# A two-layer decoder trunk on one core: transfers issued by SyncE in the order of the source

## The chip, the cores and the metric

The kernel runs on one core of one Trainium2 chip. The metric is device time in microseconds (us) of one execution. The engines named below: TensorE (PE, its weight loads PEld), VectorE (DVE), ScalarE (ACT), GpSimd (POOL) and SyncE (SP), whose only work here is to issue transfers (DMAs) and to read page numbers into its registers. All 976 transfers of this kernel are issued by SP, which the profile lists as SPq.

## The reference, cut to what matters

A prompt of 1024 rows and 8 sample rows (one new token each, 4096 earlier tokens in a paged cache) go through two layers:

```
layer 0: p = x @ w_in_ab                       # 1024 -> 3072: q, k, v, g_a, u_b, g_b
         o_a = stick_breaking(q, k, v)         # z = q k^T / 8 + bias, weights sigmoid(z) * prod(1 - sigmoid)
                                               # sample rows: k, v also from cache_k[page_table], cache_v[page_table]
         o_b = multiscale_pool(u_b) @ w_pool * pool_scale
         x = layer_norm(ALPHA * x + [o_a * silu(g_a), o_b * silu(g_b)] @ w_out_ab)
layer 1: a, a_gate, gate = split(x @ w_in_c)   # 1024 -> 3072
         h = a * sigmoid(a_gate)
         c = silu(layer_norm(depthwise_conv31(h) + b_dw))
         x = layer_norm(ALPHA * x + (c * silu(gate)) @ w_out_c)
```

Besides the rows it returns the new k and v, the last 15 rows of u_b, and the last 30 rows of h (`conv_prompt`, for the prompt). The cache of K and that of V are read as 256 pages each, one page (128 tokens x 512, 256 KB) per transfer, at addresses taken from `page_table`.

## The kernel before, in words

**Arithmetic.** A float32 product is made of three matmuls on a high and a low part: hi*hi, lo*hi, hi*lo (`project`, lines 225 to 227; `out_group`, lines 1034 to 1036). Weights come as float32 (`dma_w`, L200, tile `wraw`, 3 buffers), ACT copies the high part (L205, `whi`), POOL or DVE subtracts for the low part (L210, `wlo`). A half block of weights is 512 rows by 128 columns, 256 KB.

**Stages.** (1) Start: rows are loaded and transposed, first weights are split, small vectors are turned (`setup_small`, L479 on). (2) Input projection of layer 0 with attention, pooling and, beside it, the K pages of the cache (`decode_k`, L405 load, L417 POOL product, L409 DVE sum). (3) Output projection of layer 0 (`out_layer`). (4) From about 600 to 930 us the "V stage": the input projection of layer 1 on PE (`c_gen`, a generator over column blocks), the depthwise convolution on DVE (L1385) and, in part, on ACT and POOL (`head`, L1372 and L1375, tile `tap`), and on PE beside these the V pages (`decode_v`, L1161 load, L1163 matmuls, 9 buffers `vt`). (5) A middle piece, about 930 to 985 us: statistics, norm and gate of layer 1, with the sample rows (`sample_path`). (6) Output projection of layer 1.

**What sets the order.** One Python program calls small steps of several generators in turn: `fill.part()` is one piece of the projection (six matmuls in the V stage), `tick()` one step of `decode_k`, `decode_v` or `sample_path`, and `point()` counts down functions put off by `defer(n, fn)`, which run n points later. `manual_schedule` (L170) names the engines whose instructions keep the order in which this program calls them: PE, ACT, DVE and POOL. SP is not among them: a scheduler of the framework sets the order in which SP issues. SP issues one transfer after another; where one has to wait (for the data that it stores, or for a buffer to come free), all behind it wait too.

**Steps that the change touches.** `blocks_gen` (L229) and `c_gen` (L267) fetch half blocks of weights ahead. `tail_rows` (in `conv`, L1392 on), once for each of the 8 column blocks of layer 1, transposes the last 30 rows of h on PE (L1394), lets ACT copy them into the tile `hst` (L1396) and stores `hst` to `conv_prompt` (L1397); `hst` shares its two buffers (tag "sq") with `tap`. In `decode_v` SP reads two page numbers of each of four sequences (`page_ids`, L352, listed as TENSOR_LOAD of `pt`) and then issues 8 page loads, enough for two ticks; a tick is 4 page matmuls. `store_queries` (L382) writes the sample queries to memory (`q_dram`), from which `query_rows` (L386) reads them back. `sample_path` loads the sample rows (tile `sA`, L1249), norm vectors (L1214) and the first weight rows (`issue`, L1191, tile `vt`).

Of the kernel before, what the change touches and what calls it, by code (L numbers as in the profile page):

```python
# [24 lines left out]
P = 128  # L25
D = 1024
S = 1024
NB = 8
# [72 lines left out]
def kernel(  # L101
# [67 lines left out]

    ctx.enter_context(tc.manual_schedule(engines={ENG.PE, ENG.Activation, ENG.DVE, ENG.Pool}))  # L170
    bdw, cng, cnb = pvec[:, 0, :], pvec[:, 1, :], pvec[:, 2, :]
# [5 lines left out]
    def defer(n, fn):  # L177
        deferred.append([n, fn])
# [50 lines left out]
    def blocks_gen(blocks, chunks, tiles, when, lead):  # L229
        def src(bi, i):  # L230
            w, f0 = blocks[bi][0], blocks[bi][1]
            return w[i * 512:(i + 1) * 512, f0:f0 + P]

        stream = [(bi, i) for bi in range(1, len(blocks)) for i in range(2)]
        raws = []

        def ahead():
            if stream:
                raws.append(dma_w(src(*stream.pop(0)), 4, P))

        for _ in range(lead):
            ahead()

        def advance():
            if raws:
                nxt.append(conv_w(raws.pop(0), 4, P))
                ahead()

        for bi, b in enumerate(blocks):
            nxt = []  # L250
            for c, (c0, n) in enumerate(b[4] if len(b) > 4 else chunks):
                o = acc()[:, 0:n]
# [12 lines left out]
            tiles = nxt  # L265

    def c_gen(blocks, tiles):  # L267
# [5 lines left out]

        def fetch(bi):
            if bi < len(blocks):
                w, f0 = blocks[bi][0], blocks[bi][1]
                raws[bi] = [dma_w(w[i * 512:(i + 1) * 512, f0:f0 + P], 4, P) for i in range(2)]

        def ready(bi, i):
            if bi in raws:  # L280
                tiles.setdefault(bi, []).append(conv_w(raws[bi][i], 4, P))

        for s, (bi, c) in enumerate(items):
# [4 lines left out]
            if s == 1:  # L288
                fetch(2)
            elif s > 3 and c == 0 and bi < end:  # L290
                fetch(bi + 1)
            o = acc()[:, 0:n]
            for k in range(NK):
                project(o, tiles[bi], k, c0, n)
                if k in (1, 3, 5):
                    if s == 3 and k < 5:
                        ready(2, k // 2)
                    elif 3 < s and bi < end and (c, k) in ((0, 5), (1, 1)):
                        ready(bi + 1, c)
                    elif (bi, c, k) == (end - 1, 1, 3):  # L300
                        fetch(end + 1)
                    elif (bi, c) == (end, 0) and k < 5:
                        ready(end + 1, k // 2)
                    point()
                    yield None
# [294 lines left out]
    def evac_k(pair):  # L600
        fs = slice(pair * P, (pair + 1) * P)

        def f(c, c0, n, o):
# [7 lines left out]
            dve.tensor_tensor(out=kl, in0=o, in1=km[:, 0].bitcast(F32), op=ALU.subtract)  # L611
            sp.dma_start(km[DH:P, 1].bitcast(F32), km[DH:P, 0].bitcast(F32))
            sp.dma_start(km[0:DH, 1].bitcast(F32), kl[DH:P].bitcast(F32))

            def dup():
                sp.dma_start(km[DH:P, 0].bitcast(F32), kl[0:DH].bitcast(F32))
            defer(2, dup)

            def g():
# [8 lines left out]
                sp.dma_start(kp_out[c0:c0 + m * P, fs].rearrange("(t p) f -> p t f", p=P),  # L628
                             kst[:, 0:m * P].rearrange("p (t f) -> p t f", f=P))
                if c == 2:  # L630
                    krow = ab.tile([P, P], F32, tag="row", name="krow", bufs=3)
                    act.activation(out=krow[0:NB], in_=t[0:NB, 256:384], func=AF.Copy)
                    sp.dma_start(ks_out[:, fs], krow[0:NB])
            defer(2, g)
        return f

    def evac_v(pair):
        fs = slice(pair * P, (pair + 1) * P)

        def f(c, c0, n, o):  # L640
# [6 lines left out]
            def g():  # L647
# [8 lines left out]
                if c == 2:  # L656
                    vrow = ab.tile([P, P], F32, tag="row", name="vrow", bufs=3)
                    act.activation(out=vrow[0:NB], in_=t[0:NB, 256:384], func=AF.Copy)
                    sp.dma_start(vs_out[:, fs], vrow[0:NB])
                    sp.dma_start(vp_out[:, fs].rearrange("(t p) f -> p t f", p=P), vn)  # L660
            defer(2, g)
# [14 lines left out]
    def evac_u(g):  # L676
# [3 lines left out]
        def f(c, c0, n, o):  # L680
# [30 lines left out]
            def g2():  # L711
# [3 lines left out]
                gp.tensor_tensor(out=hb[:, 0:n], in0=hb[:, 0:n], in1=SGB[g][:, c0:c0 + n], op=ALU.mult)  # L715
                sp.dma_start(hb_dram[g * P:(g + 1) * P, c0:c0 + m], hb[:, 0:m])
                if c == 2:
                    gp.tensor_copy(shs[:, 4 + g, :], hb[:, m:n])
                if c == 2:
# [3 lines left out]
                    act.activation(out=ust[0:23], in_=t[0:23, 0:P], func=AF.Copy)  # L723
                    sp.dma_start(pool_prompt[0, 0, :, g * P:(g + 1) * P], ust[0:PS_, :])
                    sp.dma_start(pool_sample[0, :, PS_ - 1, g * P:(g + 1) * P], ust[PS_:23, :])
            defer(G2LAG, g2)
# [62 lines left out]
    def prep(pair, i):  # L789
# [4 lines left out]
        dve.tensor_tensor(out=ql, in0=q, in1=sq[:, 0].bitcast(F32), op=ALU.subtract)  # L794
        for r in (slice(0, DH), slice(DH, P)):
            sp.dma_start(sq[r, 1].bitcast(F32), sq[DH:P, 0].bitcast(F32))
        defer(2, lambda: sp.dma_start(sq[DH:P, 0].bitcast(F32), sq[0:DH, 0].bitcast(F32)))
        SQ[pair, i] = sq, ql
# [239 lines left out]
    def out_layer(w, first, ahead, X, gb, pool, finish, between, before=None, half=None, tail=None, lag=OLAG, fast0=FAST, wide=0, gps=()):  # L1038
        order = [(n4, tb) for t0 in (0, 4) for n4 in range(2) for tb in range(t0, t0 + 4)]
        for i in range(NTB + lag):  # L1040
            if i < NTB:
                order.append((2, i))
            if i >= lag:
                order.append((3, i - lag))
        dmas = {0: (1, 3)} | {9 + i: (2, i) for i in range(4)} | {13 + i: (3, i) for i in range(4)}
        convs = {i: (1, i) for i in range(4)} | {12 + i: (2, i) for i in range(4)} | {16 + i: (3, i) for i in range(4)}
# [59 lines left out]
    def before0(n4, tb):  # L1106
        if n4 == 0:
            load_res(tb + 2)
        if n4 == 0 and tb == 4:
            sp.dma_start(pool_sample[0, :, 0:PS_ - 1, :], state_pool[0, :, 1:PS_, :])  # L1110
            sp.dma_start(conv_sample[0, :, 0:KS - 1, :], state_conv[0, :, 1:KS, :])
# [18 lines left out]
    def fin0(tb, y, h):  # L1130
        sp.dma_start(x1_dram[tb * P:(tb + 1) * P, h], y[:, h])

        def f():
            for hf in range(h.start // 512, h.stop // 512):
                t = trp()
# [216 lines left out]
    def conv(cb):  # L1352
# [39 lines left out]
        def tail_rows():  # L1392
# [3 lines left out]
            act.activation(out=hst, in_=t[0:KS, 0:P], func=AF.Copy)  # L1396
            sp.dma_start(conv_prompt[0, 0, :, cb * P:(cb + 1) * P], hst)  # L1397

# [304 lines left out]
```

## Time and profile before

| | |
|---|---|
| median of 3 runs | 1111.97 us (1108.72 to 1115.1) |
| profiled execution: its time | 1110.31 us |
| its span, mean granted TensorE clock | 1108.5 us, 0.972 |
| PE busy | 1042.0 us, 94% of the span |
| DVE, POOL, ACT busy | 833.3 us (75%), 632.2 us (57%), 493.4 us (45%) |
| matmuls L225, L226, L227 | 360.3, 338.8, 339.3 us, modelled ends that overlap |
| V page matmuls L1163 | 74.5 us |
| transfers | 235.20 MB, mean 212 GB/s |

The span is the time from the first to the last instruction that the profile shows; the execution's own time is 1.8 us longer. Busy time is an average over stages: in the V stage PE has no idle time worth the name, in the start, at the layer change and in the middle piece it has. SP waits often (for POOL before weight loads, for DVE before K pages, for PE before V pages). Such a wait shows as time of another engine only where that engine wants something that stands behind the waiting transfer.

### The profile page before, as it was taken

To read this page: it belongs to the slowest core of one execution; us is meant where nothing else is said; L and a number is where in the kernel's file an instruction comes from. 1 tells how busy PE (TensorE), PEld (TensorE's weight loads), DVE (VectorE), ACT (ScalarE), POOL (GpSimd) and SP (SyncE) were. 2 spreads that over 40 slices of the span, in tenths; PEclk is the share of its full clock that TensorE was granted. 3 is DMA by queue.
4 is the path that set the end of the run, shared out by engine and by line. 5 is a ranking of instruction groups with operands and counts; after the bars stand their busy time and mean duration, and the time that the engine had idled before them with its cause. 6 is when DMAs were issued, how large, how long until landed. Compare 5 with 4: busy or idle time off the path is not lost.

```text
span 1108.5 us, 19858 instructions
## 1 busy us (share of the span) xinstructions
PE 1042.0 (94%) x6804; PEld 840.1 (76%) x6804; DVE 833.3 (75%) x982; ACT 493.4 (45%) x933; POOL 632.2 (57%) x488
## 2 busy tenths in 40 slices
PE   8899998999999989979988999999999899799996
PEld 7897887888888878979986666566666466678786
DVE  3368899899689988698874699999999960584246
ACT  5245665665766647601143244534543412462111
POOL 3266858567276878568765266757764612342135
PEclk9999999999999989989988999999999999889998
DMA  8577857865457776478425786877687678386933
GB/s 268 171 205 228 253 181 214 257 207 176 131 158 230 243 217 217 151 263 267 155 100 177 218 262 214 267 241 232 208 263 235 205 244 266 111 271 217 321 108 135
DMA packets 179350, 235.20 MB, mean 212 GB/s; under 512 B 15434, under 2 KB 95955, under 8 KB 179225
## 3 DMA queue, kind: packets, MB, share of 16 engines
q1 hardware_dynamic: 179249, 233.94, 67.0%
q8 instruction: 53, 0.87, 0.3%
q14 instruction: 48, 0.39, 0.1%
HBM read 212.60 MB, written 16.14 MB: 206 GB/s over the span
## 4 chain that ended last, share of the span: by engine, by line
PE 51%; POOL 7%; DVE 6%; DMA 5%; issue 2%; ACT 2%; SPq 2%; POOLq 0%; DVEq 0%; ACTq 0%
PE acc L225 10%; PE acc L227 9%; PE acc L226 9%; PE qv L1163 6%; DMA kt<-in_cache_k_dram 3%; POOL kt L417 2%; PE acc L1034 2%; PE acc L1036 2%; PE acc L1035 2%; DVE conv L1581 2%; PE zt L1034 1%; POOL wlo L210 1%; DVE xl L196 1%; PE qv L1199 1%; PE zt L1035 1%
## 5 line engine op out<-in xcount | busy, mean ns | idle before, releaser
L225 PE MATMUL acc<-xh,whi 128*128 128x384 f32 (+2 forms) x960 | 360.3, 375 | 1.9 <-DVE hbt L705 1.4
L227 PE MATMUL acc<-xl,whi 128*128 128x384 f32 (+2 forms) x960 | 339.3, 353 | 0.5 <-DVE xl L196 0.5
L226 PE MATMUL acc<-xh,wlo 128*128 128x384 f32 (+2 forms) x960 | 338.8, 353 | 0.0
L417 POOL TENSOR_TENSOR kt<-kt,qbs 128x1024 f32<-128x1024 f32 x96 | 237.8, 2487 | 79.0 <-DMA kt<-in_cache_k_dram 58.8
L210 POOL TENSOR_TENSOR wlo<-wraw,whi 128x512 fp32r<-128x512 f32 x122 | 163.6, 1345 | 176.6 <-ACT whi L205 154.0
L1385 DVE SCALAR_TENSOR_TENSOR conv_acc<-hbuf,wdwT,conv_acc 128x1024 f32<-128x1024 f32 x196 | 252.8, 1290 | 6.8
L225 PEld LDWEIGHTS acc<-xh,whi 128*128 128x128 f32 x960 | 183.0, 191 | 68.5 <-issue 27.2
L227 PEld LDWEIGHTS acc<-xl,whi 128*128 128x128 f32 x960 | 182.8, 190 | 18.4 <-DVE xl L196 0.9
L226 PEld LDWEIGHTS acc<-xh,wlo 128*128 128x128 f32 x960 | 183.4, 191 | 15.8
L409 DVE TENSOR_REDUCE zw<-kt 128x16 f32<-128x1024 f32 x128 | 152.9, 1211 | 28.0 <-POOL kt L417 23.0
L1375 POOL TENSOR_TENSOR conv<-conv,tap 128x512 f32<-128x512 f32 x84 | 105.9, 1293 | 15.5 <-ACT tap L1372 15.5
L205 ACT ACTIVATE whi<-wraw 128x512 fp32r<-128x512 f32 x126 | 77.6, 625 | 71.9 <-DMA wraw<-in_w_out_ab_dram 55.8
L1034 PE MATMUL acc<-whi,xh 128*128 128x256 f32 x352 | 103.9, 295 | 0.0
L1036 PE MATMUL acc<-whi,xl 128*128 128x256 f32 x352 | 101.0, 287 | 2.2 <-DVE xl L196 2.2
L1035 PE MATMUL acc<-wlo,xh 128*128 128x256 f32 x352 | 100.9, 287 | 0.6 <-POOL wlo L210 0.6
L365 DVE TENSOR_TENSOR_SCAN kp<-kp,zt 128x512 f32<-128x512 f32 (+3 forms) x96 | 92.5, 964 | 6.1 <-ACT zt L361 6.1
L1372 ACT ACTIVATE tap<-hbuf,wdwT 128x512 f32<-128x512 f32 x84 | 59.8, 721 | 46.1 <-POOL conv L1375 37.7
L1163 PE MATMUL qv<-vt,zw 128*32 128x512 f32 x512 | 74.5, 603 | 3.1 <-DMA vt<-in_cache_v_dram 3.1
L360 ACT ACTIVATE kp<-zt,nbiash 128x512 f32<-128x512 f32 (+3 forms) x96 | 55.8, 581 | 46.0 <-PE zt L823 24.5
L1034 PEld LDWEIGHTS acc<-whi,xh 128*128 128x128 f32 x352 | 68.5, 194 | 8.3 <-issue 7.8
L1036 PEld LDWEIGHTS acc<-whi,xl 128*128 128x128 f32 x352 | 68.5, 195 | 2.4 <-DVE xl L196 2.4
L1035 PEld LDWEIGHTS acc<-wlo,xh 128*128 128x128 f32 x352 | 68.5, 195 | 1.1 <-POOL wlo L210 1.0
(286 smaller groups left out, 1501.7 us busy)
## 6 DMA issues: line engine op xcount, KB each, us to landing
kt<-in_cache_k_dram SPq DMA_DIRECT2D x256, 256.0 KB
vt<-in_cache_v_dram SPq DMA_DIRECT2D x256, 256.0 KB
wraw<-in_w_in_c_dram SPq DMA_DIRECT2D x48, 256.0 KB
vt<-in_w_in_c_dram SPq DMA_DIRECT2D x48, 256.0 KB
wraw<-in_w_in_ab_dram SPq DMA_DIRECT2D x46, 256.0 KB
xt<-in_x_prompt_dram SPq DMA_DIRECT2D x8, 512.0 KB
wraw<-in_w_out_ab_dram SPq DMA_DIRECT2D x16, 256.0 KB
xres<-in_x_prompt_dram SPq DMA_DIRECT2D x8, 512.0 KB
```

Source lines behind the costliest of these rows:

```text
L210: (eng or gp).tensor_tensor(out=lo, in0=raw, in1=hi.bitcast(F32), op=ALU.subtract)
L225: pe.matmul(o, hi[:, k % 4, :], xh, start=(k == 0), stop=False)
L226: pe.matmul(o, lo[:, k % 4, :], xh, start=False, stop=False)
L227: pe.matmul(o, hi[:, k % 4, :], xl, start=False, stop=(k == NK - 1))
L409: dve.tensor_reduce(out=seg[:, j // 8, j % 8:j % 8 + 2, bi * 8:bi * 8 + 8], in_=kts.pop(s - KLAG - 1).rearrange("p a (h d) -> p a h d", d=DH),
L417: eng.tensor_tensor(out=kt, in0=kt, in1=qrow[b], op=ALU.mult)
L1034: pe.matmul(o, XH[:, k, cs], hi[:, k % 2, :], start=(k == 0), stop=False)
L1035: pe.matmul(o, XH[:, k, cs], lo[:, k % 2, :], start=False, stop=False)
L1036: pe.matmul(o, XL[:, k, cs], hi[:, k % 2, :], start=False, stop=(k == NK - 1))
L1163: pe.matmul(pv[32 * bi:32 * bi + 32, :], Z[:, j % 8 * 4 + j // 8, :], vts[bi], start=(j == 0), stop=(j == NPG - 1), tile_position=(0, 32 * ...
L1375: gp.tensor_tensor(out=ch, in0=ch, in1=tcs(t), op=ALU.add)
L1385: dve.scalar_tensor_tensor(out=part[1], in0=hb[:, j:j + S], scalar=w, in1=part[1], op0=ALU.mult, op1=ALU.add)
```

## The change

SP is added to the engines with manual order, so that it issues in the order in which the program calls `dma_start`. Many calls are put off by `defer` or moved: the K copies and stores, the pooling stores, the pair copies of the queries, the `hst` stores and the loads of the layer-1 residual; weight half blocks are asked for one at a time rather than two (`fetch(bi, i)`), and a step later. `defer(2, ...)` before the `hst` store means two points after the PE transpose. On PE, ACT, DVE and POOL the order of instructions is unchanged, and the number of transfers is the same (976).

```diff
-    ctx.enter_context(tc.manual_schedule(engines={ENG.PE, ENG.Activation, ENG.DVE, ENG.Pool}))
+    ctx.enter_context(tc.manual_schedule(engines={ENG.PE, ENG.Activation, ENG.DVE, ENG.Pool, ENG.SP}))
...
         def advance():
+            if not raws:
+                ahead()
             if raws:
                 nxt.append(conv_w(raws.pop(0), 4, P))
-                ahead()
+                defer(3, ahead)
...
-        def fetch(bi):
-            if bi < len(blocks):
-                w, f0 = blocks[bi][0], blocks[bi][1]
-                raws[bi] = [dma_w(w[i * 512:(i + 1) * 512, f0:f0 + P], 4, P) for i in range(2)]
+        def fetch(bi, i):
+            w, f0 = blocks[bi][0], blocks[bi][1]
+            raws[bi, i] = dma_w(w[i * 512:(i + 1) * 512, f0:f0 + P], 4, P)
...
             if s == 1:
-                fetch(2)
-            elif s > 3 and c == 0 and bi < end:
-                fetch(bi + 1)
+                fetch(2, 0)
+                fetch(2, 1)
...
+                    elif s == 3:
+                        fetch(3, 0)
+                    elif 3 < s and bi < end and (c, k) == (0, 1):
+                        fetch(bi + 1, 1)
                     elif 3 < s and bi < end and (c, k) in ((0, 5), (1, 1)):
                         ready(bi + 1, c)
-                    elif (bi, c, k) == (end - 1, 1, 3):
-                        fetch(end + 1)
+                        if c == 0:
+                            fetch(bi + 2, 0)
+                    elif (bi, c, k) == (end - 1, 1, 5):
+                        fetch(end + 1, 1)
...
-            sp.dma_start(km[DH:P, 1].bitcast(F32), km[DH:P, 0].bitcast(F32))
-            sp.dma_start(km[0:DH, 1].bitcast(F32), kl[DH:P].bitcast(F32))
+            def low():
+                sp.dma_start(km[DH:P, 1].bitcast(F32), km[DH:P, 0].bitcast(F32))
+                sp.dma_start(km[0:DH, 1].bitcast(F32), kl[DH:P].bitcast(F32))
+            defer(1, low)
...
-            defer(2, dup)
+            defer(3, dup)
...
-                sp.dma_start(hb_dram[g * P:(g + 1) * P, c0:c0 + m], hb[:, 0:m])
+                defer(2, lambda: sp.dma_start(hb_dram[g * P:(g + 1) * P, c0:c0 + m], hb[:, 0:m]))
...
-        for r in (slice(0, DH), slice(DH, P)):
-            sp.dma_start(sq[r, 1].bitcast(F32), sq[DH:P, 0].bitcast(F32))
-        defer(2, lambda: sp.dma_start(sq[DH:P, 0].bitcast(F32), sq[0:DH, 0].bitcast(F32)))
+        def pairs():
+            for r in (slice(0, DH), slice(DH, P)):
+                sp.dma_start(sq[r, 1].bitcast(F32), sq[DH:P, 0].bitcast(F32))
+        defer(1, pairs)
+        defer(3, lambda: sp.dma_start(sq[DH:P, 0].bitcast(F32), sq[0:DH, 0].bitcast(F32)))
...
-            sp.dma_start(conv_prompt[0, 0, :, cb * P:(cb + 1) * P], hst)
+            defer(2, lambda: sp.dma_start(conv_prompt[0, 0, :, cb * P:(cb + 1) * P], hst))
...
-            sp.dma_start(X[tb], x1_dram[tb * P:(tb + 1) * P, :])
+            defer(1, lambda tb=tb: sp.dma_start(X[tb], x1_dram[tb * P:(tb + 1) * P, :]))
```

Left out of the diff: the stores of k, v and the pooling rows, put off by 1 or 2 points in the same way; in `out_layer` of both layers the steps at which weight quarters are asked for (step 1 for 0, 13 to 17 for 12 to 16); two copies of cached rows, moved earlier; and the store of the layer-0 result, moved from before a deferred function into it.

What this makes of SP's order is shown at three places. The line numbers of the changed kernel are 5 to 9 higher: L200, L352, L382, L386, L1161, L1191, L1214, L1249 and L1397 have become L200, L357, L387, L391, L1170, L1200, L1223, L1258 and L1406.

First, SP in the V stage, around the seventh of the eight `hst` stores (out_dram<-hst) and the V pages next to it; `pt` is the page numbers, ISA sets up the address of the page load that follows, `wraw` is half a block of weights. Before:

```order
L1161 ISA
L1161 DMA vt<-in_cache_v_dram 128x512
L352 TENSOR_LOAD pt
L1161 ISA
L1161 DMA vt<-in_cache_v_dram 128x512
L1397 DMA out_dram<-hst 30x128
L200 DMA wraw<-in_w_in_c_dram 128x4x128
L352 TENSOR_LOAD pt
L1161 ISA
L1161 DMA vt<-in_cache_v_dram 128x512
```

Changed:

```order
L1170 DMA vt<-in_cache_v_dram 128x512
L200 DMA wraw<-in_w_in_c_dram 128x4x128 x2
L1406 DMA out_dram<-hst 30x128
L357 TENSOR_LOAD pt x4
L1170 ISA
L1170 DMA vt<-in_cache_v_dram 128x512
L1170 ISA
L1170 DMA vt<-in_cache_v_dram 128x512
```

Before, the reads of page numbers and the pages stood singly on both sides of the store, most of them ahead of it; now two half blocks of weights, the store, all four reads of page numbers and all eight pages of the next two ticks (the last two rows of the piece stand six times more) stand in one piece, with the store in front. At all eight `hst` stores the page numbers and the pages of the next two ticks stand right behind the store (at two of them with one half block between).

Second, SP in the start stage; `brow`, `biash`, `vst` and `wdw_n` are small vectors that PE transposes. Before (the first two `wraw` loads stand just above this piece, with one `xt` load between):

```order
L481 DMA brow<-in_sb_bias_dram 1x16x8
L482 DMA biash<-in_sb_bias_dram 128x8
L483 DMA pt<-in_page_table_dram 1x256
L491 DMA vst<-in_b_dw_dram 8x128
L491 DMA vst<-in_conv_norm_g_dram 8x128
L491 DMA vst<-in_conv_norm_b_dram 8x128
L492 DMA vst<-in_pool_scale_dram 4x128
L498 DMA nall<-in_state_conv_dram 120x2x128 x3
L200 DMA wraw<-in_w_in_ab_dram 128x4x128
L498 DMA nall<-in_state_conv_dram 120x2x128
L487 DMA wdw_n<-in_w_dw_dram 31x512
L382 DMA q_dram<-qrow 8x512
```

Changed:

```order
L560 DMA xt<-in_x_prompt_dram 128x1024 x5
L387 DMA q_dram<-qrow 8x512
L200 DMA wraw<-in_w_in_ab_dram 128x4x128 x2
L486 DMA brow<-in_sb_bias_dram 1x16x8
L487 DMA biash<-in_sb_bias_dram 128x8
L488 DMA pt<-in_page_table_dram 1x256
L492 DMA wdw_n<-in_w_dw_dram 31x512 x2
```

The store of the queries, `q_dram<-qrow`, was behind nearly all of the small vectors and now stands ahead of the first two weight half blocks, of `brow` and of both `wdw_n`.

Third, SP in the middle piece, after the last `hst` store. Before:

```order
L1191 DMA vt<-in_w_out_ab_dram 128x512
L1397 DMA out_dram<-hst 30x128
L200 DMA wraw<-in_w_out_c_dram 128x2x256
L1191 DMA vt<-in_w_out_ab_dram 128x512 x7
L200 DMA wraw<-in_w_out_c_dram 128x2x256 x2
L1191 DMA vt<-in_w_out_ab_dram 128x512
L1249 DMA sA<-in_x_sample_dram 8x256 x4
```

Changed (the rows just above this piece are the four loads of `sA` from in_x_sample_dram and six more of its norm vectors):

```order
L1223 DMA sA<-in_ln_ab_g_dram 32x256
L1223 DMA sA<-in_ln_ab_b_dram 32x256
L1200 DMA vt<-in_w_out_ab_dram 128x512 x8
L1620 DMA conv<-x_dram 128x1024
L200 DMA wraw<-in_w_out_c_dram 128x2x256 x2
L1620 DMA conv<-x_dram 128x1024
L200 DMA wraw<-in_w_out_c_dram 128x2x256 x5
L1200 DMA vt<-in_w_out_ab_dram 128x512 x8
```

The first three quarters of w_out_c (`wraw`, 128x2x256) were issued ahead of `sA`; now all of them stand behind `sA`, eight norm vectors, eight weight rows `vt` and, from the first, a residual tile `conv`.

## Rows read from the trace of the kernel before

**Rows 1.** Windows: stretch, length, busy PE PEld DVE ACT POOL, granted clock, DMA share, GB/s.

```profile
700.00:800.00 100.00, 100.00 (x503) 64.17 (x502) 97.09 (x76) 47.03 (x75) 64.34 (x57) 1.00 0.75 232
```

**Rows 2.** The view of waits: engine, line, releaser: us in total, times, longest.

```profile
DVE rmu L1540 <- PE zt L1538: 34.2, 1, 34.2
PEld qv L1163 <- DMA vt<-in_cache_v_dram: 16.5, 27, 3.3
```

**Rows 3.** Waits of SP's queue (same columns).

```profile
SPq L200 <- POOL wlo L210: 85.8, 43, 7.3
SPq L1161 <- PE qv L1163: 56.8, 39, 10.9
```

**Rows 4.** Timeline of SP's queue, 755 to 782 us: start, us, line, transfer, count.

```profile
766.69 3.72 SPq L1161 DMA_DIRECT2D vt<-in_cache_v_dram  x6
776.86 0.38 SPq L1397 DMA_DIRECT2D out_dram<-hst  x1
```

**Rows 5.** The tile hst: duration min/median/max in ns, first and last start.

```profile
L1396 ACT ACTIVATE hst<-zt x8: 249/267/268, 666.4 to 926.5; 30x128 f32<-30x128 f32 x8
```

**Rows 6.** Timeline of ACT at three copies into hst (same columns as the timeline above).

```profile
776.56 0.27 ACT L1396 ACTIVATE hst<-zt 30x128 f32<-30x128 f32 x1
813.13 0.25 ACT L1396 ACTIVATE hst<-zt 30x128 f32<-30x128 f32 x1
890.20 0.27 ACT L1396 ACTIVATE hst<-zt 30x128 f32<-30x128 f32 x1 [3.55 <-PE zt L1394]
```

**Rows 7.** Timeline of PE: the two ticks of pages after five of the copies.

```profile
671.48 1.93 PE L1163 MATMUL qv<-vt,zw 128*32 128x512 f32 x16
777.66 1.92 PE L1163 MATMUL qv<-vt,zw 128*32 128x512 f32 x16
816.20 3.24 PE L1163 MATMUL qv<-vt,zw 128*32 128x512 f32 x16
892.83 1.92 PE L1163 MATMUL qv<-vt,zw 128*32 128x512 f32 x16
931.79 2.90 PE L1163 MATMUL qv<-vt,zw 128*32 128x512 f32 x16
```

**Rows 8.** The chain that ended last, 640 to 935 us: start, us, what.

```profile
652.84 3.23 DMA vt<-in_cache_v_dram
854.74 3.54 DMA out_dram<-hst
865.10 0.47 SPq L352
866.93 3.69 DMA vt<-in_cache_v_dram
```

**Rows 9.** Timeline of PE, 862 to 874 us.

```profile
863.27 1.90 PE L1163 MATMUL qv<-vt,zw 128*32 128x512 f32 x10
867.52 1.05 PE L1163 MATMUL qv<-vt,zw 128*32 128x512 f32 x2 [2.35 <-DMA vt<-in_cache_v_dram]
872.51 0.53 PE L225 MATMUL acc<-xh,whi 128*128 128x512 f32 x1
```

**Rows 10.** Windows after two gaps of PE (columns as in rows 1).

```profile
869.20:872.60 3.40, 3.19 (x5) 0.28 (x3) 3.22 (x4) 2.39 (x4) 3.40 (x3) 0.50 0.88 274
954.50:961.30 6.80, 3.72 (x13) 3.37 (x14) 2.99 (x4) 3.83 (x10) 0.57 (x1) 0.50 0.37 134
```

**Rows 11.** Start stage: timeline of SP's queue and of PE.

```profile
27.31 0.28 SPq L382 DMA_DIRECT2D q_dram<-qrow  x1
32.85 0.55 PE L512 MATMUL zt<-ident,wdw_n 31*128 31x31 f32 x4 [2.89 <-DMA wdw_n<-in_w_dw_dram]
```

**Rows 12.** Middle piece: timeline of SP's queue and of DVE.

```profile
936.14 1.20 SPq L200 DMA_DIRECT2D wraw<-in_w_out_c_dram  x2
949.29 1.32 SPq L1249 DMA_DIRECT2D sA<-in_x_sample_dram  x4
961.21 3.10 DVE L210 TENSOR_TENSOR wlo<-wraw,whi 128x512 fp32r<-128x512 f32 x2 [3.77 <-ACT whi L205]
```

More of the change, by code (lines that the diff above doesn't have):

```diff
@@ L272, in c_gen @@
         raws, held = {}, []
-        def fetch(bi):
-            if bi < len(blocks):
-                w, f0 = blocks[bi][0], blocks[bi][1]
-                raws[bi] = [dma_w(w[i * 512:(i + 1) * 512, f0:f0 + P], 4, P) for i in range(2)]
+        def fetch(bi, i):
+            w, f0 = blocks[bi][0], blocks[bi][1]
+            raws[bi, i] = dma_w(w[i * 512:(i + 1) * 512, f0:f0 + P], 4, P)
         def ready(bi, i):
-            if bi in raws:
-                tiles.setdefault(bi, []).append(conv_w(raws[bi][i], 4, P))
+            tiles.setdefault(bi, []).append(conv_w(raws.pop((bi, i)), 4, P))
         for s, (bi, c) in enumerate(items):
@@ L627, in g @@
                 act.activation(out=kst[:, 0:m * P], in_=t[:, 0:m * P], func=AF.Copy)
-                sp.dma_start(kp_out[c0:c0 + m * P, fs].rearrange("(t p) f -> p t f", p=P),
-                             kst[:, 0:m * P].rearrange("p (t f) -> p t f", f=P))
+                defer(1, lambda: sp.dma_start(kp_out[c0:c0 + m * P, fs].rearrange("(t p) f -> p t f", p=P),
+                                              kst[:, 0:m * P].rearrange("p (t f) -> p t f", f=P)))
                 if c == 2:
@@ L632, in g @@
                     act.activation(out=krow[0:NB], in_=t[0:NB, 256:384], func=AF.Copy)
-                    sp.dma_start(ks_out[:, fs], krow[0:NB])
+                    defer(1, lambda: sp.dma_start(ks_out[:, fs], krow[0:NB]))
             defer(2, g)
@@ L658, in g @@
                     act.activation(out=vrow[0:NB], in_=t[0:NB, 256:384], func=AF.Copy)
-                    sp.dma_start(vs_out[:, fs], vrow[0:NB])
-                    sp.dma_start(vp_out[:, fs].rearrange("(t p) f -> p t f", p=P), vn)
+                    defer(1, lambda: (sp.dma_start(vs_out[:, fs], vrow[0:NB]),
+                                      sp.dma_start(vp_out[:, fs].rearrange("(t p) f -> p t f", p=P), vn)))
             defer(2, g)
@@ L723, in g2 @@
                     act.activation(out=ust[0:23], in_=t[0:23, 0:P], func=AF.Copy)
-                    sp.dma_start(pool_prompt[0, 0, :, g * P:(g + 1) * P], ust[0:PS_, :])
-                    sp.dma_start(pool_sample[0, :, PS_ - 1, g * P:(g + 1) * P], ust[PS_:23, :])
+                    defer(2, lambda: (sp.dma_start(pool_prompt[0, 0, :, g * P:(g + 1) * P], ust[0:PS_, :]),
+                                      sp.dma_start(pool_sample[0, :, PS_ - 1, g * P:(g + 1) * P], ust[PS_:23, :])))
             defer(G2LAG, g2)
@@ L1044, in out_layer @@
                 order.append((3, i - lag))
-        dmas = {0: (1, 3)} | {9 + i: (2, i) for i in range(4)} | {13 + i: (3, i) for i in range(4)}
+        dmas = {1: (1, 3)} | {9 + i: (2, i) for i in range(3)} | {13: (2, 3)} | {14 + i: (3, i) for i in range(4)}
         convs = {i: (1, i) for i in range(4)} | {12 + i: (2, i) for i in range(4)} | {16 + i: (3, i) for i in range(4)}
@@ L1108, in before0 @@
             load_res(tb + 2)
-        if n4 == 0 and tb == 4:
+        if n4 == 2 and tb == 2:
             sp.dma_start(pool_sample[0, :, 0:PS_ - 1, :], state_pool[0, :, 1:PS_, :])
@@ L1130, in fin0 @@
     def fin0(tb, y, h):
-        sp.dma_start(x1_dram[tb * P:(tb + 1) * P, h], y[:, h])
         def f():
+            sp.dma_start(x1_dram[tb * P:(tb + 1) * P, h], y[:, h])
             for hf in range(h.start // 512, h.stop // 512):
```

## Prediction

> **What bounds the kernel now.** I read the busy shares first, then the windows of each stage, the waits, the chain of waits, and last the queue of SP against PE where the two meet. In the V stage PE bounds: 100 us of it hold 100.00 us of PE work [rows 1]. DVE is nearly as full there (97.09), but at the end of the stage it waits 34.2 us in one piece for PE's statistics [rows 2], so it is ahead, and a microsecond that PE loses there is a microsecond of the end. The reader is to see next that SP spends much of its time waiting: 85.8 us before weight loads, 56.8 us before V pages [rows 3]. That is harmless as long as what stands behind the waiting transfer is needed late. PE has waited for V pages for 16.5 us in 27 pieces, 3.3 us the longest [rows 2]. So the margin between a page's landing and its first use is small in places, and a change of SP's order is judged by which page comes to stand behind which wait.
>
> SP issues in order, each transfer when the one before is issued and its own wait has ended. The order of the other engines is unchanged, so I walked the new order of SP along the old times of the others, and kept the places where something lands after its first use.
>
> **The V stage: eight stores of `hst`.** Such a store is issued when ACT has made its copy: in the profile the copy ends at 776.83 and SP starts the store at 776.86 [rows 4, 6]. The change leaves that wait and turns round what stands behind it: now the four reads of page numbers and eight pages, which are the next two ticks of PE. Before, pages of that tick were among those issued at 766.69 to 770.4 [rows 4], ten microseconds ahead of the copy. `defer(2)` doesn't put the store behind them. It runs two points after the PE transpose, two times six matmuls of some 0.2 us (503 in 100 us [rows 1]), or about 2.4 us, and the pages of the next ticks are asked for after that.
>
> From the end of the copy the eighth page lands after: the store's issue 0.4 [rows 4]; four reads of page numbers at 0.47 [rows 8], 1.9; eight page issues at 3.72/6 = 0.62 [rows 4], 5.0; landing 3.23 to 3.69 after issue [rows 8], of which I take 3.2. Sum 10.5 us. The eighth page is first read about 1.3 us after the first where the 16 matmuls of two ticks (two to a page) take 1.9 us, 2.2 and 1.8 us after it where they take 3.24 and 2.90 [rows 7]. The copies end at 666.7 and 926.8 (first and last start, plus 0.27) [rows 5], 776.8, 813.4 and 890.5 [rows 6]:
>
> | copy ends | eighth page lands | PE wants it | late |
> |---|---|---|---|
> | 666.7 | 677.2 | 671.5 + 1.3 = 672.8 | 4.4 |
> | 776.8 | 787.3 | 777.7 + 1.3 = 779.0 | 8.3 |
> | 813.4 | 823.9 | 816.2 + 2.2 = 818.4 | 5.5 |
> | 890.5 | 901.0 | 892.8 + 1.3 = 894.1 | 6.9 |
> | 926.8 | 937.3 | 931.8 + 1.8 = 933.6 | 3.7 |
>
> Together 28.8 us. At the other three stores (same two views) PE reads the first page 7.5 to 9.5 us after the copy and the eighth more than 10 us after it: nothing. From below: if the reads of page numbers cost nothing and the issue and landing go 0.8 us faster, each term falls by 2.7, and the sum is 15. From above: a landing of 3.7 makes it 31. I take 28.8, since every part of it is a row of this very queue. Nothing hides it: DVE's lead is lead over PE, and does not help PE.
>
> *Clock.* The stalls cost more than their length. After PE's gap of 2.35 us ahead of 867.52 [rows 9] the granted clock is 0.50, the lower of its two levels, 1.2 GHz, from 869.20 to 872.60; in the middle piece, after a gap of some 5 us, it is 0.50 from 954.50 to 961.30 [rows 10]. 3.4 us at half the clock are 1.7 us of work lost. Five stalls, all longer than 2.35 us, at 1.8: +9. Bounds: 0, and 14 if the lower clock lasts some 5.5 us each time.
>
> *What goes.* Before has one such stall of its own: the `hst` store issued late, at 854.74, landed 3.54 us later [rows 8]; the buffer that it held was ACT's next tap, whose POOL sum stood ahead of a weight load for which SP waited, with pages behind. PE's 16 page matmuls began at 863.27 and the next projection at 872.51 [rows 9]: 9.2 us for what takes 3.24 elsewhere [rows 7]. The store now goes out when its copy ends, seven microseconds earlier, and its pages are in time: −6. V stage together +31.8 (about +9 to +39).
>
> **Start.** The store `q_dram` waits for ACT until 27.31 [rows 11]. Before, two weight half blocks and `brow` had long been issued by then, and the first `wdw_n`, for which PE waits 2.89 us until 32.85 [rows 11], stood directly ahead of the store. Now they follow it: 27.3 + 0.3 (the store) + 1.0 to 1.2 (two weight loads, as the pair in rows 12) + three small ones at 0.3 to 0.65 come to about 30.1, where the first `wdw_n` was issued before 27.3, so it lands about 3 us later and PE waits as much longer: +3. The weights, behind POOL's split, are covered by the same wait. Bounds 0.5 (it is not the last that PE wants) and 5.5 (the loads land one behind another).
>
> **K stage and layer 0's output.** K pages mostly wait for the same DVE sums in both orders, POOL is behind them, PE is not. Some pair copies of K and Q and some weight loads go out 1 to 3 us later, where PE has idle time; some K pages go earlier. No row carries these singly: I take +1.5, with −5 and +6 as bounds from the longest single waits of PE for a V page (3.3 us [rows 2]) taken about twice either way.
>
> **Middle piece.** Before, the first quarters of w_out_c were issued at 936.14 [rows 12] or sooner. Now they stand behind the loads of `sA`, which wait for POOL's clearing of the tile until 949.29 [rows 12], eight norm vectors, eight weight rows and a residual tile. 949.3 + 1.3 [rows 12] + 17 issues at about 0.45 (between 0.33 and 0.62, rows 12 and 4) = 958.3; the eight weight rows ahead are 2.1 MB, 7.7 us at the 274 GB/s of rows 10, so the quarters land at about 964 to 966. ACT's copy of them, before done when DVE takes them at 961.21 [rows 12], ends some 4.4 us later, and DVE's chain sets the end of this piece: +4.4 (2 to 8). The last weight loads of layer 1 are moved too, by a few microseconds; PE's work on the groups of columns before them covers that, and I put them at 0 (without that cover, their own few microseconds).
>
> **Sum**, on the profiled execution's own 1110.3 us: +31.8 +3 +1.5 +4.4 = +40.7, 1151.0. The median of the runs shown is 1.7 us above that execution, within their spread of 6.4.
>
> **What the skill says against it.** What the row shows: SP's single waits last up to 7.3 and 10.9 us [rows 3], against 3.2 to 3.7 from a page's issue to its landing [rows 8]. The Trainium skill, "DMA: Bandwidth & Descriptors", section "Issuing engines are not separate DMA queues", says that the time of the sequencer to start a DMA is "usually small relative to the DMA itself". By that rule alone the order on SP would hardly matter and the time would stay at 1110. The trace agrees for the issue itself (0.62 against 3.2 us) but the rule leaves out that what a sequencer waits for is handed on to everything behind it; I give the case 5 in 100.
>
> **The rivals.**
> 1. *Stalls half as long* (1117 to 1131, worked out as the lower bounds: 15 for the pages, 5 for the clock, −6, and 0 to +3 for the rest, +14 to +17, about 1126). For it: PE's own pace between stalls gives SP time, since a stall moves the later needs but a copy may come early. Against it: PE moves ACT's copy along with its needs, so a stall at one store gives the next no more margin. 13 in 100.
> 2. *No change* (1105 to 1116, 1110): pages land before they are wanted, or DVE's lead of 34.2 us shows that the V stage has room after all. Against it, rows 1: PE has none. 5 in 100, the chance named above.
> 3. *Faster*: half blocks of weights asked for apart free SP, so that pages no longer stand behind two waiting weight loads. The price: the stall at 867.52 (−6) and most of the 16.5 us that PE has waited for pages [rows 2] go, about 1092. It decides if the copies of `hst` come so early, or the pages so late in need, that the 10.5 us fit in all eight places. Rows 7 against rows 6 say no: at 777.66 the first page is wanted 0.8 us after the copy. 5 in 100.
> 4. *Far slower* (above 1172, about 1180): each stall also delays the next weight loads on SP by the same time, so that PE stalls a second time for `wraw`; five times 5 us more. SP's longest wait for POOL before a weight load is 7.3 us [rows 3], so the room is there; but the half blocks stand ahead of the store in the new order. 9 in 100.
>
> **How the numbers follow.** The forecast, five held page groups with their clock (1131 to 1172), 68; rival 1, 13; no change 5; faster 5; rival 4, 9. What a measurement of this kernel can tell from no change is about 0.5%, 5.5 us: slower 0.90, same 0.05, faster 0.05. The range reaches to 1122, into the middle of rival 1, and to 1175, which leaves out about 2 in 10.
>
> **What would show it.** Right: in the profile of the changed kernel SP's `hst` stores each start with the end of ACT's copy, with all page loads of the next two ticks behind; PE shows five gaps of 3 to 8 us, ended by the page transfers, near the places of the table (each moved by the ones before), each with a stretch at granted clock 0.50 after it; PE's wait for `vt` rises from 16.5 to some 40 us; no gap as that at 867.52; PE's wait for `wdw_n` is about 6 us; DVE's L210 in the middle piece is about 4 us later relative to the end of the V stage. Wrong: if the pages' landing isn't what ends PE's gaps, or if the page loads' issue is spread out though the store stands ahead of them, or if the span grows in the K stage, where I put 1.5 us.

## The result and the profile after

| | before | changed |
|---|---|---|
| median | 1110.7 us (4 runs, 1108.7 to 1115.1) | 1174.1 us (4 runs, 1170.3 to 1180.4) |
| ratio | | 1.0565, 95% interval 1.0522 to 1.0607 |
| profiled execution, span, clock | 1110.31, 1108.5, 0.972 | 1180.42, 1178.7, 0.965 |

Slower by 63 us; the forecast was +41 (1151), with a range to 1175. The profiled execution of the changed kernel is the slowest of its four, so the two profiles differ by 70 us, some 7 more than the medians do.

The order of PE's matmuls is the same in both kernels, so the same matmul can be looked up in both traces. The difference of its two starts is called PE's delay here. The table shows by how much it grew in each stage; the ends of the stages are in the times of the kernel before:

| us | start (to 45) | K stage and layer-0 output (to 600) | V stage (to 940) | middle (to 985) | rest |
|---|---|---|---|---|---|
| predicted | +3 | +1.5 | +31.8 | +4.4 | 0 |
| measured | +5.3 | +17.5 | +41.5 | +5.6 | +0.2 |

The V stage first. The waits of SP, over the whole run (columns as in rows 2: us in total, times, longest):

```profile
SPq L410 <- DVE zw L414: 119.4, 54, 6.7
SPq L1170 <- PE qv L1172: 67.5, 47, 9.4
SPq L1406 <- ACT hst L1405: 45.0, 8, 11.6
SPq L200 <- POOL wlo L210: 40.8, 20, 6.1
```

The third line is the forecast's mechanism: all eight `hst` stores wait for ACT's copy, up to 11.6 us. The wait before weight loads, 85.8 us before [rows 3], halves in the order that asks for the weights later. At the fourth store, the place of the largest forecast stall, the timelines of SP, ACT and PE (start, us, engine, line, count) read, in this order:

```profile
809.46 0.40 SPq L1406 DMA_DIRECT2D out_dram<-hst  x1
812.43 4.70 SPq L1170 DMA_DIRECT2D vt<-in_cache_v_dram  x8
```

```profile
809.17 0.27 ACT L1405 ACTIVATE hst<-zt 30x128 f32<-30x128 f32 x1
```

```profile
815.43 7.13 PE L1172 MATMUL qv<-vt,zw 128*32 128x512 f32 x16 [5.09 <-DMA vt<-in_cache_v_dram]
917.53 1.92 PE L1172 MATMUL qv<-vt,zw 128*32 128x512 f32 x16
```

The copy ends at 809.44, the store starts at 809.46, the eight pages follow 2.6 us after it (the reads of page numbers), and PE, idle for 5.09 us, then takes 7.13 us for the matmuls that took 1.92 before [rows 7], since each waits for its page. The second PE row is the tick that took until 872.5 before [rows 9]: that old stall is gone. At the other four forecast places PE shows:

```profile
698.67 4.41 PE L1172 MATMUL qv<-vt,zw 128*32 128x512 f32 x12 [1.32 <-DMA vt<-in_cache_v_dram]
864.87 2.60 PE L1172 MATMUL qv<-vt,zw 128*32 128x512 f32 x4 [2.74 <-DMA vt<-in_cache_v_dram]
946.40 2.56 PE L1172 MATMUL qv<-vt,zw 128*32 128x512 f32 x4 [3.27 <-DMA vt<-in_cache_v_dram]
994.14 4.87 PE L1172 MATMUL qv<-vt,zw 128*32 128x512 f32 x12 [0.78 <-DMA vt<-in_cache_v_dram]
```

The gap in brackets is only the wait ahead of each row; the rest of the loss is in the long matmul groups. In all, PE's delay grows by 5.7, 10.4, 6.8, 8.6 and 5.3 us at the five places, 36.8 us with what the clock takes; forecast were 4.4, 8.3, 5.5, 6.9 and 3.7 and 9 for the clock, 37.8. PE's view of the same over the whole run, and the windows (columns as in rows 1), of which the first is 100 us around the fourth store and the others are stretches of low clock:

```profile
DVE rmu L1549 <- PE zt L1547: 64.9, 1, 64.9
PEld qv L1172 <- DMA vt<-in_cache_v_dram: 52.7, 67, 3.7
PE qv L1172 <- DMA vt<-in_cache_v_dram: 16.4, 12, 5.1
```

```profile
765.00:865.00 100.00, 91.80 (x419) 55.77 (x418) 92.09 (x73) 37.00 (x62) 51.81 (x46) 0.96 0.57 179
813.40:820.20 6.80, 4.77 (x10) 0.93 (x11) 6.62 (x6) 0.00 (x0) 0.71 (x1) 0.50 0.89 302
864.60:868.00 3.40, 2.93 (x5) 0.54 (x6) 3.26 (x3) 2.18 (x4) 2.47 (x3) 0.50 0.97 278
946.50:949.90 3.40, 3.16 (x6) 0.43 (x8) 0.00 (x0) 0.00 (x0) 0.16 (x1) 0.50 0.90 303
```

PE is busy for 91.80 of the 100 us, where a stretch of the same stage before held 100.00 [rows 1]. DVE's wait for PE's statistics grew from 34.2 [rows 2] to 64.9 us: DVE was ahead, and could not absorb what PE lost. The granted clock was low at the second, third and fourth of the five stalls, for 6.8, 3.4 and 3.4 us, so at most 6.8 us of work were lost together, against 1.7 in this stage before.

PE also lost time where no store stands ahead: 2.7 us at 702 to 704 in the time of the kernel before, and 3.2 us at 808 to 810. SP's timeline of the changed kernel, ahead of these two places:

```profile
719.39 4.57 SPq L200 DMA_DIRECT2D wraw<-in_w_in_c_dram  x2
726.27 4.70 SPq L1170 DMA_DIRECT2D vt<-in_cache_v_dram  x8
838.89 4.74 SPq L200 DMA_DIRECT2D wraw<-in_w_in_c_dram  x2
845.94 4.72 SPq L1170 DMA_DIRECT2D vt<-in_cache_v_dram  x8
```

The second half block of each pair waits for POOL (3.7 and 3.9 us), and the eight pages stand behind it. At two more such places, where PE loses 1.2 us (at 656) and 3.4 us (at 880), SP has no wait for a half block: there a page waits for PE to free a buffer (at most 3.6 and 3.1 us), with the next pages behind it.

The start, from SP's timeline (the first row is that of the kernel before, the second that of the changed kernel) and from PE's (changed kernel):

```profile
26.52 0.29 SPq L487 DMA_DIRECT2D wdw_n<-in_w_dw_dram  x1
31.44 0.60 SPq L492 DMA_DIRECT2D wdw_n<-in_w_dw_dram  x2
```

```profile
33.32 0.19 PE L510 MATMUL zt<-ident,brow 1*128 1x1 f32 x1 [2.35 <-DMA brow<-in_sb_bias_dram]
38.11 0.60 PE L517 MATMUL zt<-ident,wdw_n 31*128 31x31 f32 x4 [4.60 <-DMA wdw_n<-in_w_dw_dram]
```

The middle piece, from the timelines of SP, DVE and PE:

```profile
1013.61 1.36 SPq L1258 DMA_DIRECT2D sA<-in_x_sample_dram  x4
1023.16 0.97 SPq L200 DMA_DIRECT2D wraw<-in_w_out_c_dram  x2
```

```profile
1031.52 1.37 DVE L210 TENSOR_TENSOR wlo<-wraw,whi 128x512 fp32r<-128x512 f32 x2 [9.75 <-ACT whi L205]
```

```profile
1039.65 0.58 PE L1044 MATMUL acc<-whi,xh 128*128 128x256 f32 x1 [6.93 <-ACT whi L205]
```

PE now waits for `brow` as well, 2.35 us, and 4.60 for `wdw_n` (2.89 before [rows 11]). `wdw_n` is issued 4.9 us later than before, and PE starts on it 6.7 us after its issue, where it was 6.3 us (32.85 [rows 11]). That gives the whole delay; the wait for `brow` ends before `wdw_n` lands and adds nothing to it. The quarters of w_out_c are issued at 1023.16, 9.55 us after the first load of `sA`, where the sum had 9.0; DVE waits 9.75 us for them where it waited 3.77 [rows 12].

### The profile page after: what moved, and what is told of

The parts are those of the page before. It is cut to its first block, busy times and chain, and to the rows that moved or that the text cites. A ratio compares the mean times of both kernels' runs of the same rounds, so it can differ in the third digit from the quotient of the medians.

```text
span 1178.7 us, 19829 instructions
## 1 busy us (share of the span) xinstructions
PE 1076.8 (91%) x6804; PEld 846.5 (72%) x6804; DVE 834.7 (71%) x982; ACT 494.8 (42%) x933; POOL 629.4 (53%) x488
## 4 chain that ended last, share of the span: by engine, by line
PE 45%; DVE 16%; DMA 14%; POOL 7%; issue 7%; SPq 6%; ACT 4%; DVEq 0%; POOLq 0%; ACTq 0%
PE acc L225 9%; PE acc L227 8%; PE acc L226 8%; PE qv L1172 7%; DVE zw L414 4%; DMA kt<-in_cache_k_dram 4%; DMA vt<-in_cache_v_dram 3%; DVE kp L370 3%; POOL conv L1384 2%; DMA qh<-qh 2%; SPq L410 2%; DVE kt L422 2%; PE acc L1044 1%; DVE xl L196 1%; SPq L357 1%
## 5 line engine op out<-in xcount | busy, mean ns | idle before, releaser
L422 POOL TENSOR_TENSOR kt<-kt,qbs 128x1024 f32<-128x1024 f32 x96 | 234.5, 2452 | 84.1 <-DMA kt<-in_cache_k_dram 62.0
L1172 PE MATMUL qv<-vt,zw 128*32 128x512 f32 x512 | 102.3, 617 | 16.6 <-DMA vt<-in_cache_v_dram 16.4
L1172 PEld LDWEIGHTS qv<-vt,zw 128*32 128x32 f32 x512 | 19.2, 109 | 78.5 <-DMA vt<-in_cache_v_dram 52.7
```

What stands on the lines that cost most here:

```text
L422: eng.tensor_tensor(out=kt, in0=kt, in1=qrow[b], op=ALU.mult)
L1172: pe.matmul(pv[32 * bi:32 * bi + 32, :], Z[:, j % 8 * 4 + j // 8, :], vts[bi], start=(j == 0), stop=(j == NPG - 1), tile_position=(0, 32 * ...
```

## The experiments

Of each, the growth of PE's delay by stage is taken from its profile as above; the kernel before had medians of 1109.7 to 1111.8 us in these runs. A profile is one execution, and the times are medians: the profiled execution lay between 5.2 us below its kernel's median (g3_sched_actq) and 6.3 us above it (changed).

| us | start | K, layer 0 | V stage | middle | time | ratio (95%) |
|---|---|---|---|---|---|---|
| changed | +5.3 | +17.5 | +41.5 | +5.6 | 1174.1 | 1.0565 (1.0522 to 1.0607) |
| e1_sched | −0.8 | −2.6 | +2.7 | 0.0 | 1104.6 | 0.9946 (0.9924 to 0.9969) |
| e2_hst6 | +4.6 | +15.4 | +6.2 | +6.5 | 1138.3 | 1.0234 (1.0196 to 1.0272) |
| e3_prep | +4.8 | +12.0 | +41.9 | +5.7 | 1174.7 | 1.0564 (1.0510 to 1.0618) |
| e4_startmid | −4.2 | +11.5 | +40.5 | +0.6 | 1161.0 | 1.0465 (1.0433 to 1.0496) |
| f1_comb | −3.9 | +18.5 | +4.3 | +1.6 | 1128.8 | 1.0160 (1.0125 to 1.0194) |
| f2_actq | −5.2 | +6.9 | +4.7 | +0.9 | 1120.1 | 1.0099 (1.0069 to 1.0129) |
| f3_hybrid | +0.6 | +1.3 | +5.2 | +1.0 | 1115.8 | 1.0043 (1.0014 to 1.0072) |
| g1_hst_act | +4.6 | +11.9 | +4.9 | +5.3 | 1140.3 | 1.0271 (1.0234 to 1.0308) |
| g2_actq_hst | −4.6 | +7.4 | +3.5 | +0.4 | 1117.5 | 1.0097 (1.0058 to 1.0136) |
| g3_sched_actq | −1.3 | +4.5 | −0.4 | −0.7 | 1117.3 | 1.0072 (1.0045 to 1.0100) |
| h1_start | −4.2 | +4.6 | +1.5 | −1.4 | 1106.3 | 0.9974 (0.9949 to 0.9999) |
| h2_sched_again | +0.5 | −3.8 | +3.7 | −1.4 | 1109.9 | 0.9999 (0.9976 to 1.0023) |

**e1_sched and h2_sched_again: is it the order, or the later calls?**

```diff
-    ctx.enter_context(tc.manual_schedule(engines={ENG.PE, ENG.Activation, ENG.DVE, ENG.Pool, ENG.SP}))
+    ctx.enter_context(tc.manual_schedule(engines={ENG.PE, ENG.Activation, ENG.DVE, ENG.Pool}))
```

> The changed kernel with SP taken out of the manual order again; all moved and put-off calls stay. Theory (the loss is in the order in which SP issues, not in the calls being put off): the framework's scheduler again puts the pages ahead of the waiting stores and copies, and the time comes back to 1105 to 1120 us; PE's waits for V pages fall from 69 us (52.7 + 16.4) to about 20. Rival (the calls themselves are asked for too late, whoever orders them): 1145 to 1174 us, with most of the V stage's +41 us still there.

Measured: 1104.6 us; PE's loader waits 20.9 us for V pages, PE 3.3. With the same calls and the same transfers, SP's order alone is worth 64 to 70 us (1174.1 against 1109.9, the run that follows, and 1104.6). The calls being put off cost nothing in sum that can be measured. Run again with more rounds:

> e1_sched once more, with more rounds: 1104.6 us before, 0.9946 of the kernel before. If that gain is real: 0.992 to 0.998 again; if it was the day's spread: the interval takes in 1.0.

Measured: 1109.9, interval across 1.0. The first run's half per cent did not come back; the two together say: no difference from before that can be told. The small losses of the V stage are in part here too: PE loses 2.1 and 2.5 us at 702 to 704, and 2.3 and 3.0 us at 808 to 810, in e1_sched and h2_sched_again.

**e2_hst6 and g1_hst_act: is it the store that holds the pages?**

```diff
-            defer(2, lambda: sp.dma_start(conv_prompt[0, 0, :, cb * P:(cb + 1) * P], hst))
+            defer(6, lambda: sp.dma_start(conv_prompt[0, 0, :, cb * P:(cb + 1) * P], hst))     # e2_hst6
+            act.dma_start(conv_prompt[0, 0, :, cb * P:(cb + 1) * P], hst)                      # g1_hst_act
```

> The changed kernel with only the eight hst stores put off by 6 points instead of 2, which puts them behind the page loads of the next two ticks in SP's queue. Theory (the store's wait for ACT's copy holds the pages): the five large PE stalls of the V stage (5.7, 10.4, 6.8, 8.6, 5.3 us) go, and so does most of the low clock after them; the V stage loses about 10 us instead of 41 against before, time about 1140 us (1135 to 1148). Rival (pages are late because SP waits for POOL before weight half blocks, or for PE's buffers, and the store is a bystander): PE's stalls only move, time 1160 to 1176.

> The changed kernel with the eight hst stores issued by ACT right behind its copy; everything on SP else as in the changed kernel. Theory (the store's wait in SP's queue is what holds the pages): the five stalls go as with the store put off, and the store also frees its buffer at once: V stage +5 us against before instead of +41, time 1137 us (1131 to 1143). Rival (the eight late places need SP to issue the pages earlier, with or without the store): 1155 to 1175 us.

Measured: 1138.3 and 1140.3, both as the theory has it; the V stage loses 6.2 and 4.9 instead of 41.5 us. Two different ways of taking the store out from in front of the pages give the same, so the store is what held them. The largest single loss that is left is the stall at 777.7 in the time of the kernel before: 5 of its 10.4 us stay in both. SP's and PE's timelines of e2_hst6 there:

```profile
787.40 6.43 SPq L200 DMA_DIRECT2D wraw<-in_w_in_c_dram  x2
796.10 4.72 SPq L1170 DMA_DIRECT2D vt<-in_cache_v_dram  x8
800.93 0.41 SPq L1406 DMA_DIRECT2D out_dram<-hst  x1
```

```profile
802.58 4.05 PE L1172 MATMUL qv<-vt,zw 128*32 128x512 f32 x10 [0.31 <-DMA vt<-in_cache_v_dram]
```

The two half blocks wait for POOL's split of earlier ones (the second until 793.4), and the pages, whose buffers had been free since 787, stand behind them. So the rival had a part here: a second holder of pages, hidden by the first.

**e3_prep: are late query copies what the K stage loses?**

```diff
-        defer(1, pairs)
-        defer(3, lambda: sp.dma_start(sq[DH:P, 0].bitcast(F32), sq[0:DH, 0].bitcast(F32)))
+        pairs()
+        defer(2, lambda: sp.dma_start(sq[DH:P, 0].bitcast(F32), sq[0:DH, 0].bitcast(F32)))
```

> The changed kernel with the copies of the queries called as before the change (pairs at once, the last copy 2 points later instead of 1 and 3). Theory (the unforeseen +17 us before the V stage come from query copies that stand behind K pages that wait for DVE): PE's waits for qh fall from 8.5 us to under 3, and the first projection of the V stage starts about 8 us earlier than in the changed kernel: time about 1166 us (1160 to 1169). Rival (SP is held by ACT's query copy instead, K pages come later, POOL and DVE pass it on): 1172 to 1185 us.

Measured: 1174.7 us, no gain. PE's waits for `qh` did fall from 8.5 to 0.9 us, but PE then waits 6.6 us for DVE's part of K. The theory falls: taking away the wait that PE shows only moved it. The time is that of the rival.

**e4_startmid: the start and the middle piece.**

```diff
-        sp.dma_start(q_dram, row[0:NB, :])
+        defer(2, lambda: sp.dma_start(q_dram, row[0:NB, :]))
...
     def sample_path():
+        LATE.extend(dma_quarter(w_out1, 0, i) for i in range(2, 4))    # ahead of the loads of sA
...
-    late1 = load_first(w_out1, range(2, 4), dx, dve, ("whi1", "wlo1"), 2)
+    late1 = [conv_w(raw, 2, 256, dx, dve, ("whi1", "wlo1"), 2) for raw in LATE]
```

> The changed kernel with two moves: the q_dram store behind the small vectors in the start, and the first two quarters of w_out_c ahead of the loads of sA in the middle piece. Theory (both terms as predicted): PE's delay at the end of the start falls from 5.3 us to about 1, that of the middle piece from some 6 to 7 us to about 1, time about 1163 us (1159 to 1167). Rival (other loads take their place: small state rows late in the start, sample rows in the middle): 1169 to 1177 us.

Measured: 1161.0 us. Both terms go, as the theory has it, and the start comes out 4.2 us ahead of before, whose own wait for `wdw_n` (2.89 us [rows 11]) is gone too.

**f1_comb and f2_actq: do the terms add, and what is left before the V stage?** f1_comb has the edits of e2_hst6 and e4_startmid; f2_actq has those and the following, with the stores of `kst`, `krow`, `vrow` and `vn` moved to ACT in the same way:

```diff
-                sp.dma_start(km[DH:P, 1].bitcast(F32), km[DH:P, 0].bitcast(F32))       # in low(), put off by 1
+            act.dma_start(km[DH:P, 1].bitcast(F32), km[DH:P, 0].bitcast(F32))          # at once
...
-                sp.dma_start(sq[r, 1].bitcast(F32), sq[DH:P, 0].bitcast(F32))          # pairs, put off by 1
+                act.dma_start(sq[r, 1].bitcast(F32), sq[DH:P, 0].bitcast(F32))         # at once
```

> The changed kernel with both repairs: the hst stores put off by 6 points, and the two moves of the start and the middle piece. If the terms add (V stage -36, start and middle -13 from the two kernels timed before, 1174): 1125 us (1120 to 1130). What is left against before's 1110 is then the 11 to 18 us between the start and the V stage. If they don't add (the stages hide each other's stalls): above 1133.

> f1_comb with the first copies of K and of the queries, and the stores of k and v, issued by ACT right behind the ACT instruction that makes their data, so that SP's queue holds no wait for ACT there. Theory (before the V stage the time goes where SP waits for ACT's or DVE's copies with K pages behind): the loss from 45 us to the first projection of the V stage falls from 11 to 18 us to under 6, time about 1115 us (1109 to 1120). Rival (the K pages pace themselves through their four buffers, and SP's waits for copies only take the place of its waits for DVE): the loss stays above 10 us, and ACT pays for about 70 issues: 1122 to 1135.

Measured: 1128.8, so the terms add within 4 us, and what is left is mostly the K stage; 1120.1 with ACT's queue, where the loss between the start and the V stage falls from 18.5 to 6.9 us in the profiles. SP's waits from 50 to 503 us of the changed kernel, and from 40 to 490 us of f2_actq:

```profile
SPq L410 <- DVE zw L414: 104.0, 42, 6.7
SPq L805 <- ACT qh L801: 18.7, 4, 9.2
```

```profile
SPq L410 <- DVE zw L414: 122.1, 48, 5.6
SPq L808 <- DMA qh<-qh: 22.2, 3, 13.3
```

In f1_comb, from which f2_actq differs by ACT's transfers alone, the two waits of the changed kernel are 106.1 and 20.4 us. In f2_actq SP no longer waits for ACT's queries; it waits more for DVE to free a K buffer, that is, it stands ready earlier. The waits for `qh` that remain (L808) are those of one copy for another. The gain of 8.7 us falls just short of the theory: the loss was to be under 6 us and the time at most 1120. 68 transfers went to ACT's queue, so SP was rid of their issue time as well as of the waits; the two were not separated. The size of the K-stage term is known only roughly: in profiles whose SP order is the same in the K stage it was 11.5, 11.9, 15.4, 17.5 and 18.5 us.

**f3_hybrid, g2_actq_hst, g3_sched_actq and h1_start: a version that beats both?** f3_hybrid takes ENG.SP into the manual order only from the V stage on, with the edits of f1_comb; g2_actq_hst is f2_actq with `hst` on ACT; g3_sched_actq is e1_sched with the ACT issues of g2_actq_hst; h1_start is e1_sched with SP in source order up to the first K page and the `q_dram` edit of e4_startmid.

> SP ordered by the framework's scheduler up to the end of layer 0 and by the source from the V stage on, with the hst stores put off by 6 points and the first quarters of w_out_c ahead of sA. By the sum of stages: -3 us up to 600 us (as with the scheduler throughout), +6 in the V stage (as with hst stores put off), 0 in the middle: 1113 us (1107 to 1119). If a source order of SP can be as good as the scheduler's in the V stage too: 1104 to 1107.

> f2_actq with the hst stores on ACT as well, instead of put off by 6 points. If the store is all that is left to win in the V stage: its loss there falls from about 5 us to 0 or below, 1114 us (1109 to 1118). If what is left there are pages behind weight half blocks that wait for POOL: 1118 to 1122, as f2_actq.

> The scheduler's order on SP with the moved calls (1104.6 when timed before), and ACT issuing the copies and stores of the kernel f2_actq and the hst stores. If SP's waits for ACT still cost something in the scheduler's order: 1096 to 1102 us. If the scheduler had already put other transfers ahead of them: 1103 to 1110, and ACT's extra issues may cost a little.

> The scheduler's order on SP with the moved calls (as e1_sched), but SP in source order up to the first K page, with the q_dram store behind the small vectors there. If the gain of the start (PE reaches its first K-stage matmuls 4 us earlier than before in e4_startmid) lasts: 1100 us (1097 to 1103). If the K stage takes it back, since K pages pace it: 1104 to 1108.

Measured: 1115.8, 1117.5, 1117.3 and 1106.3 us. The stages add in f3_hybrid. In g2_actq_hst the V stage still loses 3.5 us, which fits pages behind half blocks better than a last cost of the store; its time lies 0.5 us from the border between the two forecasts and does not decide. Under the scheduler's order ACT's issues win nothing (g3_sched_actq): the time is longer than either forecast had it, by 7 us at the least, and why stays open, since its stages come from an execution 5.2 us below the median. Of the four only h1_start is below before, 0.9974, with an interval that ends at 0.9999. In its profile the start is 4.2 us ahead and the K stage takes that back, but that execution was 4.8 us above the median. No version here beats before by more than this measurement can tell.

## Why the prediction was right, and where not

*The number.* 1174.1 lies in the range by 0.9 us, and outside the band of the forecast's own mechanism (1131 to 1172). That it lies inside is luck: the K stage took 17.5 us where its bound was +6, and so the prediction's own sign of being wrong, a span that grows in the K stage, came.

*V stage, five stalls: right.* Place, order and size hold (36.8 us with the clock, forecast 37.8), and two experiments remove most of them with the store. The split is off, and the sum comes so near in part by luck. At the first and fifth place, where the clock did not fall, the stalls were 1.3 and 1.6 us longer than forecast. The clock fell at three places, not five, and took at most 6.8 us in place of 9. The gaps ahead of the matmuls were also smaller than the 3 to 8 us that were to show it (0.78 to 5.09 us in the rows above), since PE reads page by page as they land.

*V stage, what goes: right,* −7.4 for −6, at the place named.

*V stage, missed: +12 us.* After two of the other three stores PE loses 0.7 and 1.5 us, and at four places without a store ahead 1.2, 2.7, 3.2 and 3.4. The step that failed is the sum over stores alone. Half blocks that wait for POOL hold pages too, as e2_hst6 shows at the fourth store and SP's rows above at two of the four places (2.7 and 3.2 us); at the other two pages wait behind a page that waits for a buffer. Since e1_sched and h2_sched_again lose 2.1 to 3.0 us at those first two places, most of that needs no source order of SP; which of the moved calls brings it was not tried.

*Start: mechanism right, +5.3 for +3,* near its upper bound. The issue of `wdw_n` was put 3 us later and came 4.9 us later: it had gone out at 26.52, earlier than the sum took it, and the store ahead of it now started at 28.47 in place of 27.31, since PE was 1.1 us late by 13 us, before the two orders differ.

*K stage: wrong, +17.5 for +1.5, past the bound of +6.* The step that failed is "K pages mostly wait for the same DVE sums in both orders, POOL is behind them, PE is not". SP's order put waits for ACT's and DVE's copies ahead of K pages. e1_sched shows that the order causes the loss, and f2_actq that SP's waits for ACT, with the issue time of those transfers, are a large part of it; PE's visible waits, 8.5 us for `qh`, were not (e3_prep). How the delay reaches PE is argued and not shown: POOL and DVE take the pages in order, and PE's scores and evacuations need DVE. What the remaining 7 us of f2_actq are stays open.

*Middle: right,* +5.6 for +4.4, and e4_startmid removes it.

*The skill's rule.* With the same transfers from the same engine, order was worth 64 to 70 us (e1_sched, h2_sched_again), and eight stores of 0.4 us issue time were worth 34 us when ACT issued them (g1_hst_act), and 36 us when SP issued them later (e2_hst6). What was gained is a wait taken out of the way, far more than the 3.2 us of eight issues. The Trainium skill, "DMA: Bandwidth & Descriptors", section "Issuing engines are not separate DMA queues", weighs only the time to start a DMA against the DMA. The measurement decides against reading that as a bound.

*The rivals.* "Far slower" came nearest by its number (1172 and more), but not by its mechanism: no second stall for weights followed each first. The excess over the forecast came from the K stage, priced at +1.5, and from places of the V stage that were not priced at all.

## What to carry to other kernels

When a queue that issues in order is given a new order, look for each wait in it and ask which transfer behind it is wanted soonest; eight small stores cost more here (34 to 36 us) than all other moved transfers together, and putting them four steps later, or on another engine's queue, won that back. Sum over every kind of wait, not only the worst: when the store was out of the way, the weight loads ahead of the same pages were the next holder. And in a stage whose engines feed one another in a ring (page, product, sum, free buffer), don't take the wait that PE shows for the price: in e3_prep 7.6 us of it went, and the time stayed.

## What the runs showed that was not expected

The clock did not fall after every stall: in one profile, gaps at PE of 5.09, 2.74 and 3.27 us were followed by 0.50, and 16 page matmuls drawn out over 7.5 us with no gap above 1.32 or 0.78 us (the first and fifth place) were not. Whether a start 4 us earlier shortens the run by as much is open: in the profile of h1_start its 4.2 us were lost again by 600 us (+0.4 there), but by the medians h1_start is 3.9 us shorter than before, and e1_sched, with no earlier start to speak of (0.8 us), came out 5.7 us shorter and, run again, 0.3.
